# Turning attention probabilities and queries with VectorE and DRAM scratches, in a hybrid SSD and attention trunk

## The chip, the cores and the metric

The kernel runs on one core of one Trainium2 chip. The core has five engines, each with its own instruction queue that is worked off in order: TensorE (PE; its weight loads have a row of their own, PEld), VectorE (DVE), ScalarE (ACT), GpSimd (POOL) and SyncE (SP). DMA transfers are issued from SP, ACT or POOL and run on 16 shared DMA engines. The metric is device time in microseconds; lower is better. The time before is 1022.89 us, the median of three runs (1022.04 to 1023.73).

## The reference

Batch 1, 256 tokens, width 2048, two layers, all in float32. Layer A is a Mamba-2 SSD mixer, layer B a sliding-window attention with grouped queries and a sink for each head. The change is in layer B alone:

```python
proj = x @ w_in                                   # 2048 -> [2048 q | 2048 gate]
q = rope(proj[..., :2048] + q_bias)               # 32 heads of 64; 4 K/V heads, 8 query heads each
k, v = rope(x @ kv_w + kv_b)                      # K and V shared, 4 heads of 64 (rope on k only)
s = einsum("qd,kd->qk", q, [k_prev | k_own]) / 8  # blocks of 128 queries, 256 keys
valid = (diff >= 0) & (diff < 128) & (kpos >= 0)  # diff = query position - key position
m = maximum(max(where(valid, s, -inf)), sink)
p = exp(s - m) / (sum(exp(s - m)) + exp(sink - m))
o = (p @ [v_prev | v_own]) * silu(gate)
x = layernorm(alpha * x + o @ w_out)
```

With 128 queries in a block and a window of 128, query t of a block sees keys 0 to t of its own block and keys t+1 to 127 of the block before: 128 keys in all. The first block has no block before it.

## The kernel before

Products with weights are done in split precision: each float32 weight and activation is split into a high part (float32r) and the rest, and three matmuls (high by high, high by rest, rest by high) are added in PSUM. Weights come in units of 128 partitions by 2048 elements (1 MB), as two DMAs from SP into five raw buffers. `load_unit` (L120) has ScalarE write the high part (L133) and VectorE the rest (L134). `next_unit` (L179) keeps two units ahead of TensorE.

Layer B (from L717) first makes keys and values (`kT`, `vt`), then works through `B_ORDER` (L39), a list of twelve blocks of four units each: "q" (`q_block`, L750: queries of K/V group j, tokens stationary, L712 to L714), "g" (`gate_block`, L778: L195 to L197) and "o" (output projection, `out_unit`, L255 to L257, added to the residual on VectorE at L260 and L264). The last "o" block is run by `out_last`, with the layer norm behind it.

Attention of group j is put between those units by a list of delayed calls: `later(n, fn)` (L201) runs fn at the n-th `tick` (L204) from then, and there is one tick after each unit. Program order sets the order of each engine's queue, except that the Tile scheduler may move an instruction that isn't ready behind others of its engine. The steps for group j and half h (the 128 query tokens of half 0 or 1) are:

- `qtr` (L764), one tick after the q block: four 128 x 128 TensorE transposes (L767) into a PSUM tile `ax`, and a scaled copy to `qT` on ScalarE (L771).
- `attend(j, 0)` (L792), two ticks after the q block, and `attend(j, 1)` three ticks later (one for the last group): scores (L804) of eight heads over nk = 128 (h = 0) or 256 (h = 1) keys; the mask added on VectorE while PSUM is emptied (L809); maximum (L817); eight exponentials with row sums on ScalarE (L823); normalisation (L828).
- `turn_p` (L832), three ticks after `attend`: eight TensorE transposes for h = 0, sixteen for h = 1 (L837), emptied by VectorE (L844) and ScalarE (L842) into tiles `pt`.
- `pv` (L847), one to three ticks later: the product with values (L851), two matmuls of 512 columns for each block of 128 keys, then gate and split (L857, L866, L867) into `oH`, `oL`, which the "o" block of the group uses as stationary operand.

PSUM tiles `ax` have four buffers of one bank. Bias rows are the only DMAs of POOL in these blocks (L690).

Of the kernel before, what the change touches and what calls it, by code (L numbers as in the profile page):

```python
# [38 lines left out]
B_ORDER = [("q", 0), ("g", 0), ("q", 1), ("g", 1), ("o", 0), ("q", 2), ("g", 2), ("o", 1),  # L39
           ("q", 3), ("g", 3), ("o", 2), ("o", 3)]  # L40
# [17 lines left out]
def trunk(ctx: ExitStack, tc: tile.TileContext, A: dict, out: bass.AP, dbg=None):  # L58
# [31 lines left out]
    mask_a1 = cc[:, 640:896]  # L90
# [630 lines left out]
    for h in range(2):  # L721
# [22 lines left out]
        later(2, ktr)  # L744

# [4 lines left out]
    def q_block(j):  # L750
        pss = [mm_tile(), mm_tile()]
        qb = bias_row(A["qb"][j * 512 : (j + 1) * 512])
        for ui in range(4):
            u = next_unit()
            for h in range(2):
                x_stat(pss[h], h, u, ui)
            tick()
        for h in range(2):
            qt = bp.tile([P, 8, 64], F32, tag="qt", name=nm("qt"), bufs=2)
            qf = qt[:].rearrange("p a d -> p (a d)")  # L760
            nc.vector.tensor_tensor(qf, pss[h][:], qb[:], ALU.add)
            rope(qt[:], h, 8)

            def qtr(h=h, qf=qf):  # L764
                pt = ax_tile()
                for p_ in range(4):
                    nc.tensor.transpose(  # L767
                        pt[:, p_ * P : (p_ + 1) * P], qf[:, p_ * P : (p_ + 1) * P], ident
                    )
# [21 lines left out]

    def attend(j, h):  # L792

        nk = P * (h + 1)
        q2 = qT[j, h]
        p = bp.tile([P, 8, nk], F32, tag=f"p{h}", name=nm("p"), bufs=1)
        mask = mask_a1 if h else mask_a0
        per = 512 // nk
        for b in range(0, 4, per):
# [8 lines left out]
            for par in range(2):  # L808
                nc.vector.tensor_tensor(  # L809
                    p[:, par * 4 + b : par * 4 + b + per, :],  # L810
                    pss[par][:].rearrange("p (a k) -> p a k", a=per),
                    mask.unsqueeze(1).to_broadcast([P, per, nk]), ALU.add,
                )
# [14 lines left out]
        nc.vector.tensor_tensor(p[:], p[:], ri.unsqueeze(2).to_broadcast([P, 8, nk]), ALU.mult)  # L828

        pts = {}  # L830

        def turn_p():  # L832
            for kc in range(h + 1):
                for par in range(2):
                    pt = ax_tile()
                    for a in range(4):
                        nc.tensor.transpose(  # L837
                            pt[:, a * P : (a + 1) * P], p[:, par * 4 + a, kc * P : (kc + 1) * P], ident
                        )
                    t = bp.tile([P, 512], F32, tag="pt", name=nm("pt"), bufs=4)  # L840
                    if par:
                        nc.scalar.copy(t[:], pt[:])  # L842
                    else:
                        nc.vector.tensor_copy(t[:], pt[:])  # L844
                    pts[kc, par] = t

        def pv():  # L847
            ov = ax_tile()
            for kc in range(h + 1):
                for par in range(2):  # L850
                    nc.tensor.matmul(  # L851
                        ov[64 * par : 64 * par + 64, :], vt[:, kc, j * 64 : j * 64 + 64], pts[kc, par][:],
# [17 lines left out]
        later(3, turn_p)  # L870
        later(4 if last or h else 6, pv)
# [25 lines left out]
    def done2(h):  # L897
        mv, rs = norm_scale(bp, st2, h)
        if h:
# [7 lines left out]
            for c in range(4):  # L907
# [3 lines left out]
                t = bp.tile([P, 512], F32, tag="pt", name=nm("t"), bufs=4)  # L911
# [11 lines left out]
        for c in range(4):  # L923
            sl = slice(c * 512, (c + 1) * 512)
            v = xr[:, h, sl]
            t = bp.tile([P, 512], F32, tag="pt", name=nm("t"), bufs=4)
# [100 lines left out]
```

## Time and profile before

| what | value |
|---|---|
| time, median of three runs | 1022.89 us |
| span of the profiled execution, first to last instruction | 1022.1 us |
| TensorE matmul / weight load, busy | 1001.7 us (98%) / 905.5 us (89%) |
| VectorE / ScalarE / POOL, busy | 774.2 (76%) / 562.8 (55%) / 89.8 us (9%) |
| mean granted TensorE clock | 0.999 |
| DMA | 199.31 MB, mean 195 GB/s |

The profiled execution's own time is its span of 1022.1 us; the median of the runs is 0.8 us above it. A profile row names line, engine and operation, output tile and input tiles, shape, and count; behind the bar stand busy time and mean duration (ns), and behind the second bar the idle time of the engine just before these instructions and what ended it. In the order of time a row begins with start and duration in us, and "[0.42 <-ACT pt L842]" says that the engine stood idle for 0.42 us until that ScalarE instruction had ended. Matmul durations overlap: a matmul's row lasts from its start to its modelled end, while the next has begun.

### The profile page before, as it was taken

How to read it: one execution, taken by the hardware profiler on the slowest of the kernel's cores; microseconds unless marked ns; L12 is line 12 of the kernel's file. 1: busy time of each engine (PE TensorE's matmuls, PEld its weight loads, DVE VectorE, ACT ScalarE, POOL GpSimd, SP SyncE). 2: the span in 40 equal slices, each digit the busy share in tenths (PEclk: the TensorE clock that was granted, in tenths of full speed). 3: DMA queues.
4: the chain of work that ended last, by engine and by line, in shares of the span. 5: the costliest groups of instructions: out<-in, count | busy, mean ns of one | idle time of the engine just before them, and what ended most of it. 6: DMA issues, size and time to landing. Idle time of an engine off the chain costs nothing. (4 is left out here: it accounts for less than half of the span.)

```text
span 1022.1 us, 17627 instructions
## 1 busy us (share of the span) xinstructions
PE 1001.7 (98%) x7028; PEld 905.5 (89%) x7028; DVE 774.2 (76%) x1106; ACT 562.8 (55%) x924; POOL 89.8 (9%) x112
## 2 busy tenths in 40 slices
PE   7999999999999999999999999999999999999997
PEld 7999899999998998999999999868988879879975
DVE  6868887876886787696786787798577785785776
ACT  6585857637655655664663763535545453453642
POOL 0000303004003002100300300301000000000002
PEclk9999999999999999999999999999999999999999
DMA  8786676575666666656656556647655445545522
GB/s 308 249 299 246 204 245 195 171 233 169 211 218 191 218 195 204 205 188 202 208 179 218 156 190 210 227 146 232 197 167 169 156 140 183 173 140 183 194 96 82
DMA packets 57794, 199.31 MB, mean 195 GB/s; under 512 B 6304, under 2 KB 10672, under 8 KB 56944
## 3 DMA queue, kind: packets, MB, share of 16 engines
q1 hardware_dynamic: 56352, 192.14, 57.3%
q0 software_dynamic: 1072, 5.53, 1.5%
q8 instruction: 55, 0.90, 0.4%
q10 hardware_dynamic: 288, 0.52, 0.1%
q14 instruction: 27, 0.22, 0.1%
HBM read 195.93 MB, written 2.23 MB: 194 GB/s over the span
## 5 line engine op out<-in xcount | busy, mean ns | idle before, releaser
L134 DVE TENSOR_TENSOR wl<-wr,wh 128x1024 fp32r<-128x1024 f32 (+2 forms) x342 | 398.3, 1181 | 135.4 <-ACT wh L133 134.0
L133 ACT ACTIVATE wh<-wr 128x1024 fp32r<-128x1024 f32 (+2 forms) x342 | 337.4, 1011 | 238.9 <-PE mm L196 77.1
L195 PE MATMUL mm<-xH,wh 128*128 128x256 f32 x1296 | 361.2, 279 | 8.0 <-ACT wh L153 6.0
L197 PE MATMUL mm<-xH,wl 128*128 128x256 f32 x1296 | 359.8, 278 | 2.1 <-DVE wl L134 2.1
L196 PE MATMUL mm<-xL,wh 128*128 128x256 f32 x1296 | 360.1, 278 | 0.0
L195 PEld LDWEIGHTS mm<-xH,wh 128*128 128x128 f32 x1296 | 244.6, 189 | 10.2 <-ACT wh L153 6.3
L197 PEld LDWEIGHTS mm<-xH,wl 128*128 128x128 f32 x1296 | 244.5, 189 | 2.7 <-DVE wl L134 2.7
L196 PEld LDWEIGHTS mm<-xL,wh 128*128 128x128 f32 x1296 | 244.7, 189 | 1.1
L255 PE MATMUL mm<-wh,yH 128*128 128x512 f32 x256 | 101.4, 396 | 0.0
L256 PE MATMUL mm<-wh,yL 128*128 128x512 f32 x256 | 99.9, 390 | 0.0
L257 PE MATMUL mm<-wl,yH 128*128 128x512 f32 x256 | 99.7, 390 | 0.0
L492 POOL TENSOR_TENSOR yz<-yz,z 128x256 f32<-128x256 f32 x32 | 32.9, 1036 | 532.0 <-DVE yz L487 532.0
L195 PE MATMUL mm<-x1H,wh 128*128 128x256 f32 x256 | 71.9, 281 | 0.0
L197 PE MATMUL mm<-x1H,wl 128*128 128x256 f32 x256 | 71.0, 277 | 0.0
L196 PE MATMUL mm<-x1L,wh 128*128 128x256 f32 x256 | 71.0, 277 | 0.0
L359 DVE SCALAR_TENSOR_TENSOR cv<-mm,pc,cv 128x255 f32<-128x255 f32 x144 | 68.6, 476 | 1.4
L712 PE MATMUL mm<-wh,x1H 128*128 128x512 f32 x160 | 63.3, 396 | 0.0
L714 PE MATMUL mm<-wl,x1H 128*128 128x512 f32 x160 | 62.6, 392 | 0.3 <-DVE wl L134 0.2
L713 PE MATMUL mm<-wh,x1L 128*128 128x512 f32 x160 | 62.6, 391 | 0.2 <-DVE x1L L676 0.2
L255 PEld LDWEIGHTS mm<-wh,yH 128*128 128x128 f32 x256 | 48.1, 188 | 10.3 <-DVE z L429 1.0
L257 PEld LDWEIGHTS mm<-wl,yH 128*128 128x128 f32 x256 | 48.1, 188 | 10.2
L256 PEld LDWEIGHTS mm<-wh,yL 128*128 128x128 f32 x256 | 48.1, 188 | 9.0
(180 smaller groups left out, 1306.2 us busy)
## 6 DMA issues: line engine op xcount, KB each, us to landing
wr<-in_wa SPq DMA_DIRECT2D x158, 512.0 KB, 5.0
wr<-in_wo SPq DMA_DIRECT2D x64, 512.0 KB, 4.8
wr<-in_wq SPq DMA_DIRECT2D x32, 512.0 KB, 4.5
wr<-in_wg SPq DMA_DIRECT2D x32, 512.0 KB, 5.2
wr<-in_wb SPq DMA_DIRECT2D x32, 512.0 KB, 4.6
rb<-rscr SPq DMA_DIRECT2D x16, 512.0 KB, 5.4
el<-rscr SPq DMA_DIRECT2D x16, 256.0 KB, 4.8
wr<-in_wkv SPq DMA_DIRECT2D x8, 512.0 KB, 4.3
```

Source lines behind the costliest of these rows:

```text
L133: nc.scalar.activation(h[:, sl], raw, AF.Copy)
L134: nc.vector.tensor_tensor(l[:, sl], raw, h[:, sl].bitcast(F32), ALU.subtract)
L195: nc.tensor.matmul(ps, ah, bh, start=first, stop=False)
L196: nc.tensor.matmul(ps, ah, bl, start=False, stop=False)
L197: nc.tensor.matmul(ps, al, bh, start=False, stop=last)
L255: nc.tensor.matmul(ps[:], aH[:, k, hs], u.h[:, ks], start=k == 0, stop=False)
L256: nc.tensor.matmul(ps[:], aL[:, k, hs], u.h[:, ks], start=False, stop=False)
L257: nc.tensor.matmul(ps[:], aH[:, k, hs], u.l[:, ks], start=False, stop=k == 3)
L359: nc.vector.scalar_tensor_tensor(a[:, sft:], ps[:, : S - sft], w(3 - sft), a[:, sft:], ALU.mult, ALU.add)
L712: nc.tensor.matmul(ps[:], x1H[:, kk, hs], u.h[:, ks], start=kk == 0, stop=False)
L713: nc.tensor.matmul(ps[:], x1L[:, kk, hs], u.h[:, ks], start=False, stop=False)
L714: nc.tensor.matmul(ps[:], x1H[:, kk, hs], u.l[:, ks], start=False, stop=kk == KT - 1)
```

## The change

Three things change in layer B.

- *Turning.* Queries and probabilities are no longer transposed by TensorE. VectorE transposes them in blocks of 32 x 32 (`nc.vector.transpose`) into an SBUF tile; four DMAs from POOL, one for each group of 32 partitions, write that to a DRAM scratch (`to_dram`) in an order in which one more DMA from POOL reads it back with keys (or head dimensions) on partitions. The queries' scaled copy on ScalarE then reads the loaded tile instead of PSUM. A call to the loads (`load_q`, `load_p`) comes two ticks behind the stores.
- *128 scores a row in both halves.* For half 1 the scores over 256 keys are still made, but one row of 128 is kept: ScalarE copies the scores of the own block (128 columns), and VectorE overwrites those with key index above the query's by the scores of the block before (`copy_predicated`). Maximum, exponentials and normalisation then run over 128. The value product uses `vt[:, 1] - vt[:, 0]`, formed once: all probabilities by the values of the block before, plus the probabilities masked with `tri` (one multiplication on VectorE) by the difference. The number and the size of its matmuls stay; their moving operand is read in runs of 32 elements.
- *Order and delays.* `B_ORDER` puts q2 ahead of o0 and q3 ahead of o1. `attend(j, 0)` comes four ticks after the q block, `turn_p` two ticks after `attend`, `load_p` four, `pv` six (seven for the last group).

The tiles `p0`, `p1` and `pt` (20 KB a partition together) give way to five buffers of 4 KB under one tag `pb`; temporaries of the last layer norm move from `pt` to the tags `qt` and `qT`.

```diff
-B_ORDER = [("q", 0), ("g", 0), ("q", 1), ("g", 1), ("o", 0), ("q", 2), ("g", 2), ("o", 1),
-           ("q", 3), ("g", 3), ("o", 2), ("o", 3)]
+B_ORDER = [("q", 0), ("g", 0), ("q", 1), ("g", 1), ("q", 2), ("o", 0), ("g", 2), ("q", 3),
+           ("o", 1), ("g", 3), ("o", 2), ("o", 3)]
...
-    mask_a1 = cc[:, 640:896]
+    tri = cc[:, 256:384]
...
+    nc.vector.tensor_tensor(vt[:, 1, :], vt[:, 1, :], vt[:, 0, :], ALU.subtract)
...
-            def qtr(h=h, qf=qf):
-                pt = ax_tile()
-                for p_ in range(4):
-                    nc.tensor.transpose(
-                        pt[:, p_ * P : (p_ + 1) * P], qf[:, p_ * P : (p_ + 1) * P], ident
-                    )
-                q2 = bp.tile([P, 4, P], F32, tag="qT", name=nm("qT"), bufs=2)
-                nc.scalar.activation(
-                    q2[:], pt[:].rearrange("p (a t) -> p a t", a=4), AF.Copy, scale=0.125
-                )
-                qT[j, h] = q2
-
-            later(1, qtr)
+            def turn_q(h=h, qf=qf):
+                z = bp.tile([P, 1024], F32, tag="pb", name=nm("zq"), bufs=5)[:, :512]
+                nc.vector.transpose(
+                    z.rearrange("p (c a t) -> p a c t", c=4, a=4), qf.rearrange("p (a c d) -> p a c d", a=4, c=4)
+                )
+                d = to_dram(z, 128, "qd")
+
+                def load_q():
+                    t = bp.tile([P, 8, 4, 32], F32, tag="pb", name=nm("qr"), bufs=5)[:, :4]
+                    nc.gpsimd.dma_start(t.rearrange("p b a t -> p b (a t)"), d[:].rearrange("b p f -> p b f"))
+                    q2 = bp.tile([P, 4, P], F32, tag="qT", name=nm("qT"), bufs=2)
+                    nc.scalar.activation(
+                        q2[:].rearrange("p a (b t) -> p a b t", b=4), t.rearrange("p b a t -> p a b t"),
+                        AF.Copy, scale=0.125,
+                    )
+                    qT[j, h] = q2
+
+                later(2, load_q)
+
+            later(1, turn_q)
...
+    def to_dram(z, n, name):
+
+        t = dram.tile([4, P, n], F32, tag=name, name=nm(name), bufs=2)
+        for a in range(4):
+            nc.gpsimd.dma_start(
+                t[a, :, :].rearrange("(b t) f -> t b f", b=4),
+                z[32 * a : 32 * a + 32, :].rearrange("p (b f) -> p b f", b=4),
+            )
+        return t
+
     def attend(j, h):
 
+        q2 = qT[j, h]
+        p = bp.tile([P, 8, P], F32, tag="pb", name=nm("p"), bufs=5)
         nk = P * (h + 1)
...
-                nc.vector.tensor_tensor(
-                    p[:, par * 4 + b : par * 4 + b + per, :],
-                    pss[par][:].rearrange("p (a k) -> p a k", a=per),
-                    mask.unsqueeze(1).to_broadcast([P, per, nk]), ALU.add,
-                )
+                v = p[:, par * 4 + b : par * 4 + b + per, :]
+                sv = pss[par][:].rearrange("p (a k) -> p a k", a=per)
+                if h:
+                    nc.scalar.copy(v, sv[:, :, P:])
+                    nc.vector.copy_predicated(
+                        v, mask_a0.bitcast(I32).unsqueeze(1).to_broadcast([P, per, P]), sv[:, :, :P]
+                    )
+                else:
+                    nc.vector.tensor_tensor(v, sv, mask_a0.unsqueeze(1).to_broadcast([P, per, P]), ALU.add)
...
         def turn_p():
-            for kc in range(h + 1):
-                for par in range(2):
-                    pt = ax_tile()
-                    for a in range(4):
-                        nc.tensor.transpose(
-                            pt[:, a * P : (a + 1) * P], p[:, par * 4 + a, kc * P : (kc + 1) * P], ident
-                        )
-                    t = bp.tile([P, 512], F32, tag="pt", name=nm("pt"), bufs=4)
-                    if par:
-                        nc.scalar.copy(t[:], pt[:])
-                    else:
-                        nc.vector.tensor_copy(t[:], pt[:])
-                    pts[kc, par] = t
+            z = bp.tile([P, 1024], F32, tag="pb", name=nm("z"), bufs=5)
+            nc.vector.transpose(
+                z[:].rearrange("p (b h q) -> p h b q", b=4, h=8), p[:].rearrange("p h (b k) -> p h b k", b=4)
+            )
+            held["d"] = to_dram(z, 256, "pd")
+
+        def load_p():
+            t = bp.tile([P, 4, 8, 32], F32, tag="pb", name=nm("pT"), bufs=5)
+            nc.gpsimd.dma_start(t[:].rearrange("p a h q -> p a (h q)"), held["d"][:].rearrange("a p f -> p a f"))
+            held["p"] = [t]
+            if h:
+                m = bp.tile([P, 4, 8, 32], F32, tag="pb", name=nm("pm"), bufs=5)
+                nc.vector.tensor_tensor(
+                    m[:], t[:],
+                    tri.rearrange("p (a q) -> p a q", a=4).unsqueeze(2).to_broadcast([P, 4, 8, 32]), ALU.mult,
+                )
+                held["p"].append(m)
...
-                        ov[64 * par : 64 * par + 64, :], vt[:, kc, j * 64 : j * 64 + 64], pts[kc, par][:],
+                        ov[64 * par : 64 * par + 64, :], vt[:, kc, j * 64 : j * 64 + 64],
+                        held["p"][kc][:, :, 4 * par : 4 * par + 4, :].rearrange("p a h q -> p h a q"),
...
-        later(3, turn_p)
-        later(4 if last or h else 6, pv)
+        later(2, turn_p)
+        later(4, load_p)
+        later(7 if last else 6, pv)
...
-            later(2, lambda j=j: attend(j, 0))
+            later(4, lambda j=j: attend(j, 0))
```

More of the change, by code (lines that the diff above doesn't have):

```diff
@@ L925, in done2 @@
             v = xr[:, h, sl]
-            t = bp.tile([P, 512], F32, tag="pt", name=nm("t"), bufs=4)
+            t = bp.tile([P, 512], F32, tag=("qt", "qT")[c % 2], name=nm("t"), bufs=2)
             nc.vector.scalar_tensor_tensor(
```

9 lines of the change are left out of this document (3 added, 6 removed).

## The prediction

> **What bounds the kernel now.** I read the page first, then the busy times of the stretch from the first gate block of layer B to its last output block, then groups by line, and last the order of time around each interruption of TensorE.
>
> ```profile
> span 1022.1 us, 17627 instructions
> PE 1001.7 (98%) x7028; PEld 905.5 (89%) x7028; DVE 774.2 (76%) x1106; ACT 562.8 (55%) x924; POOL 89.8 (9%) x112
> ...
> 715.80:1011.60 295.80, 294.69 (x1796) 249.83 (x1794) 211.64 (x323) 141.41 (x290) 6.79 (x8) 1.00 0.47 157
> ```
>
> The last row's columns are TensorE, weight loads, VectorE, ScalarE, POOL, granted clock, DMA share, GB/s. In the 295.8 us that the change touches, TensorE lacks 1.1 us of being busy throughout at a granted clock of 1.00; VectorE has 72%, the DMA engines 47%, POOL 2%. So time in layer B is TensorE's issue time, and what leaves TensorE's queue shortens the span unless something becomes late. Layer A keeps its code.
>
> Busy TensorE isn't its price, though: matmuls overlap. The price of a group is the step from its first start to the next group's first start.
>
> ```profile
> 805.55 0.40 PE L255 MATMUL mm<-wh,oH 128*128 128x512 f32 x1
> 811.02 1.03 PE L837 MATMUL ax<-cc,p 128*128 128x128 f32 x8
> 811.99 2.71 PE L804 MATMUL ax<-kT,qT 64*128 64x256 f32 x16
> 813.56 0.73 PEld L804 LDWEIGHTS ax<-kT,qT 64*128 64x128 f32 x6 [0.42 <-ACT pt L842]
> 814.62 0.50 PE L255 MATMUL mm<-wh,oH 128*128 128x512 f32 x1
> ...
> 777.69 1.97 PE L837 MATMUL ax<-cc,p 128*128 128x128 f32 x16
> 779.41 0.37 PE L195 MATMUL mm<-x1H,wh 128*128 128x256 f32 x1
> ...
> 732.26 1.04 PE L767 MATMUL ax<-cc,qt 128*128 128x128 f32 x8
> 733.05 0.36 PE L195 MATMUL mm<-x1H,wh 128*128 128x256 f32 x1
> 738.88 1.16 PE L804 MATMUL ax<-kT,qT 64*128 64x128 f32 x16
> ...
> 953.33 2.00 PE L804 MATMUL ax<-kT,qT 64*128 64x256 f32 x16
> 955.25 0.39 PE L195 MATMUL mm<-x1H,wh 128*128 128x256 f32 x1
> ...
> 973.72 1.53 PE L837 MATMUL ax<-cc,p 128*128 128x128 f32 x12
> 976.22 0.66 PE L837 MATMUL ax<-cc,p 128*128 128x128 f32 x4 [0.96 <-DVE o L857]
> 976.63 0.48 PE L255 MATMUL mm<-wh,oH 128*128 128x512 f32 x1
> ```
>
> A weight unit is 811.02 - 805.55 = 5.47 us of TensorE; one tick of the delay list is one unit.
>
> **What leaves TensorE.**
>
> ```profile
> L837 PE MATMUL ax<-cc,p 128*128 128x128 f32 x96 | 12.2, 275 | 1.0 <-DVE o L857 1.0
> L767 PE MATMUL ax<-cc,qt 128*128 128x128 f32 x32 | 4.2, 274 | 0.0
> L851 PE MATMUL ax<-pt,vt 128*64 128x512 f32 x48 | 12.1, 609 | 0.0
> ```
>
> - The 96 transposes of probabilities (L837). First half, 8 of them: 811.99 - 811.02 = 0.97 us. Second half, 16: 779.41 - 777.69 = 1.72. In the last block the second half takes 976.63 - 973.72 = 2.91, its last four waiting 0.96 for VectorE. With the last block's first half near 0.8 (like the eight at 732.26): 3 x 0.97 + 0.8 + 3 x 1.72 + 2.91 = 11.8 us.
> - The 32 transposes of queries (L767): 733.05 - 732.26 = 0.79 a group, four groups: 3.2 us. The two group rows bear both out: 12.2 + 4.2 busy plus 1.0 idle, less some 0.2 us by which each of twelve groups' last matmul overlaps what follows, is 15.0.
> - Scores of the second half. Directly behind transposes they take 814.62 - 811.99 = 2.63 us, with a wait for the ScalarE copy that frees a PSUM buffer; in the last block, with buffers free, 955.25 - 953.33 = 1.92. The change puts no transposes ahead of them and still does 16 matmuls of 256 columns: 3 x 0.71 = 2.1 us.
> - An interruption less. The unit between queries' transposes and scores takes 738.88 - 733.05 = 5.83 instead of 5.47. About half of the 0.36 I give to the transposes ahead of it (bounds 0 and 0.36): 4 x 0.2 = 0.8 us.
>
> Sum: 11.8 + 3.2 + 2.1 + 0.8 = 17.9 us off TensorE's queue.
>
> By the Trainium skill ("TensorE: Matmul & The Clock Gate", Part 4: PE-mode transpose) a transpose takes about 275 ns in a kernel's context. The mean column here reads 275 and 274 too; by that, 128 of them would be an estimated 35 us and the time near 988. The starts, 0.10 to 0.12 us apart (0.97/8, 1.72/16), decide against it.
>
> **What VectorE and ScalarE get.**
>
> ```profile
> L809 DVE TENSOR_TENSOR p<-ax,cc 128x512 f32<-128x512 f32 x24 | 15.3, 679 | 1.3 <-PE ax L804 1.3
> L817 DVE TENSOR_REDUCE sm<-p 128x8 f32<-128x2048 f32 x4 | 9.1, 2284 | 0.1
> L828 DVE TENSOR_TENSOR p<-p,sm 128x2048 f32<-128x2048 f32 x4 | 9.2, 2290 | 0.1
> L828 DVE TENSOR_TENSOR p<-p,sm 128x1024 f32<-128x1024 f32 x4 | 4.9, 1216 | 0.0
> L844 DVE COPY pt<-ax 128x512 f32<-128x512 f32 x12 | 8.1, 680 | 0.0
> L788 DVE SCALAR_TENSOR_TENSOR sg<-sg,mm 128x256 f32<-128x256 f32 x16 | 6.5, 405 | 1.6 <-ACT sg L787 1.4
> L842 ACT COPY pt<-ax 128x512 f32<-128x512 f32 x12 | 6.5, 574 | 0.0
> L787 ACT ACTIVATE sg<-mm 128x256 f32<-128x256 f32 x16 | 5.9, 367 | 0.0
> L823 ACT ACTIVATE p<-p,sm 128x256 f32<-128x256 f32 x32 | 15.8, 496 | 21.8 <-DVE sm L819 21.8
> L823 ACT ACTIVATE p<-p,sm 128x128 f32<-128x128 f32 x32 | 12.4, 388 | 16.6 <-DVE sm L819 16.6
> ```
>
> VectorE loses L844 (8.1), 16 of the 24 mask additions (16 x 0.679 = 10.9) and half of the 2048-wide reduce and normalisation (9.1/2 + 9.2/2 = 9.2): 28.2 us. No row shows a block transpose or a predicated copy. Nearest by size and type: 1.216 for 1024 elements, 0.680 for 512, 0.405 for 256 out of PSUM. Eight transposes of probabilities, eight of queries, four extra multiplications and 16 predicated copies: 9.7 + 5.4 + 4.9 + 6.5 = 26.5 us; the one subtraction on the values is another 0.4. So VectorE stays near 211 us. At the low end a transpose costs half its row, at the high end four times it (+45 us: 256 of some 279 us, still under TensorE). I take the rows, as size and type agree. ScalarE: minus 6.5 and 32 x 0.108 = 3.5, plus 16 x 0.367 = 5.9. All of this lies beside TensorE.
>
> **What the round trip through DRAM costs.** Each turn issues four stores and one load on POOL: 16 turns, 80 issues, 12.6 MB both ways; with the 46.4 MB of the stretch (157 GB/s x 295.8 us) that is 59 MB in 279 us, 211 GB/s, and layer A ran with TensorE full at such rates.
>
> ```profile
> L690 POOL DMA_DIRECT2D bias<-in_qb x4 | 2.1, 537 | 69.6 <-DVE qt L761 68.9 <-DVE vt L732 0.7
> out<-xr SPq DMA_DIRECT2D x6, 256.0 KB, 2.3
> bias<-in_qb POOLq DMA_DIRECT2D x4, 256.0 KB, 4.6
> wr<-in_wg SPq DMA_DIRECT2D x32, 512.0 KB, 5.2
> ...
> 757.44 1.16 PEld L804 LDWEIGHTS ax<-kT,qT 64*128 64x128 f32 x10 [0.17 <-PE ax L837]
> 769.79 2.28 DVE L828 TENSOR_TENSOR p<-p,sm 128x2048 f32<-128x2048 f32 x1
> ...
> 982.26 1.94 PE L851 MATMUL ax<-pt,vt 128*64 128x512 f32 x8
> 986.11 0.68 DVE L867 TENSOR_TENSOR oL<-o,oH 128x512 fp32r<-128x512 f32 x1
> ```
>
> An issue took 0.54 us on POOL, a store of 256 KB landed after 2.3, loads of 256 and 512 KB after 4.6 and 5.2. The store and load shapes are new; bounds are 0.54 for an issue with as many pieces as the bias row and 2.1 for a load with four times the pieces, landing of a store 2.3 to 4.6. I take 0.54 and the longer landing.
>
> - Probabilities, turn to use: transpose 1.2, four issues 2.2, landing 4.6, issue 0.5, landing 5.2, multiplication 1.2: 14.9 us against four ticks, 21.9. Hidden.
> - Queries of blocks 0 and 3, turn to first score: transpose 0.7, eight issues 4.3 (both halves' stores stand ahead of the load), rest of the landing 2.4, issue 0.5, landing 4.6, ScalarE 0.6 (L787's and L842's rows): 13.1 against three ticks, 16.4. Hidden.
> - Queries of blocks 1 and 2 queue on POOL behind the previous block's second half, turned at the same tick. Its probabilities were ready 769.79 + 2.28 - 757.44 = 14.6 us after the scores' start, now 3.0 earlier (1.1 each for reduce and normalisation, as L828's two rows differ, and 8 x 0.108): 11.6, or 6.1 after the query block's end. Transpose to 7.3, twelve issues to 13.8, two load issues to 14.9, landing 4.6 to 7.2 (half a 512 KB load beside it), ScalarE 0.6: 20.1 to 22.7 against four ticks plus the values' matmuls between (4 x 12.1 / 48 = 1.0), 22.9. That just fits; with long load issues (2.1) it is 3 us late. I take 0.5 each, 1.0 us in all (bounds 0 and 6).
> - The last block's second half now reaches its values' matmuls one unit later, directly ahead of the last output block. Before, L867 ended at 986.79, 2.6 us after those matmuls (982.26 + 1.94); the output block has 2.7 us of first-half matmuls to do meanwhile. I take 0.3 (bounds 0 and 1.5, one weight split in front).
>
> What waits behind a late load: on ScalarE the queries' copy, on VectorE the multiplication, each with weight splits behind it that TensorE reads two units (10.9 us) later; a wait of a few microseconds stays inside that.
>
> Sum: 17.9 - 1.0 - 0.3 = 16.6 us. Profiled span 1022.1 - 16.6 = 1005.5; the median of the runs shown, 1022.89, lies 0.8 above that span, so **1006.3 us**.
>
> **Rivals.**
> - *Part of the gain is eaten* by queries that come late for blocks 1 and 2 and a stall at the last output block: the upper bounds above, 6 + 1.5 instead of 1.3, make 1012.5. For it: new shapes of DMA, the thin margin. Against it: VectorE runs ahead of the ticks where nothing holds it. It takes 2.4 times that lateness (17.9 / 7.5) to reach no change.
> - *POOL's queue becomes the bound: slower than before.* If each issue waits out the VectorE instruction under way (1.22 us, the L828 row), it costs 1.76: twelve stores and two loads for blocks 1 and 2 take 14 x 1.22 = 17.1 us more, less at most 2.8 of margin, so 14 us or more late twice; blocks 0 and 3 take ten issues, 12.2 more less 3.3, 8.9 late twice. That is +46 on -17: 1051. It turns into a loss at some 0.55 us more an issue (2 x (14 x 0.55 - 2) + 2 x (10 x 0.55 - 3.3) = 16). Against it: all bias rows were issued in 0.54 beside a VectorE at 72%. The Trainium skill ("SBUF — State Buffer", Who interferes with whom) says that VectorE in a two-port mode shuts POOL out of SBUF while it writes descriptors, and gives 3.1 us instead of 0.62 for such a DMA; no row here shows a large instruction of that kind beside a POOL issue, so whether the block transpose is one stays open.
> - *The values' matmuls read slower*, as they now take runs of 32 elements with gaps in place of 512 in a row. At twice the 12.1 us of L851 the time is 1018.4; the loss begins at 2.4 times. No row speaks for it.
> - *Nothing moves*: the transposes' slots turn into waits of the same length for data that comes through DRAM, 1022.9. Against it stand the margins above.
>
> **How the numbers follow.** No change means within 0.2%, 1020.8 to 1024.9, about what a measurement of this kernel can tell. The forecast (1003 to 1009) has 0.62, the eaten gain 0.17, the slower reads 0.03, nothing moved 0.05, POOL's queue 0.13. Faster is 0.62 + 0.17 + 0.03 = 0.82, same 0.05, slower 0.13. The lower end of the range, 1003, is the whole 17.9 with up to 2 us more from interruptions that go; the upper end, 1018, takes in the eaten gain and slower reads.
>
> **What would show it.** L837 and L767 gone, 6900 matmuls; scores of the second half near 1.9 us each; TensorE still above 99% busy in layer B, with waits before L804 of blocks 1 and 2 under 1 us; POOL issues of 0.5 us, VectorE's transposes near 1.2 and 0.7. Wrong if TensorE waits for the ScalarE copy of the queries or for the loaded probabilities by more than 5 us together, or if POOL's issues take over 1 us.

## The result and the profile after

The changed kernel takes **1010.73 us** (median of four runs, 1009.90 to 1011.93) against 1022.75 (1022.04 to 1023.73, four runs beside it). The ratio is 0.9885 with a 95% interval of 0.9871 to 0.9899: 12.0 us faster. The forecast was 1006.3, its range 1003 to 1018. Line numbers below are those of the changed kernel: scores L821, value products L876, queries' copy L776, the multiply `pm` L866, gate and rounding of the result L883, L892, L893, stores L804, loads L862 (probabilities) and L774 (queries), block transposes L855 and L767.

From the page of the changed kernel:

```profile
span 1010.1 us, 17539 instructions
...
PE 989.0 (98%) x6900; PEld 891.8 (88%) x6900; DVE 772.3 (76%) x1115; ACT 558.9 (55%) x928; POOL 138.1 (14%) x192
```

The 128 transposes are gone (7028 matmuls before). The profiled execution took 1011.93 us, the slowest of the four; its span is 12.0 us below that of the kernel before, as the medians are. Where the time went is read from three stretches of layer B, cut at starts on TensorE: the first transpose of the keys, the start of the unit behind the last gate matmul, the first matmul of the tail. Columns as in the prediction's first windows row; the third number is the length. The kernel before:

```profile
715.02:960.82 245.80, 245.66 (x1574) 211.70 (x1572) 171.59 (x272) 120.63 (x251) 1.07 (x2) 1.00 0.50 164
960.82:1011.59 50.77, 49.81 (x230) 38.90 (x228) 40.33 (x53) 21.56 (x40) 5.71 (x6) 1.00 0.35 124
1011.59:1022.12 10.53, 3.97 (x9) 1.34 (x8) 5.82 (x10) 2.07 (x5) 1.10 (x1) 0.90 0.43 156
```

The changed kernel:

```profile
713.98:947.22 233.24, 232.03 (x1470) 199.04 (x1468) 169.74 (x283) 119.15 (x272) 44.41 (x76) 1.00 0.65 213
947.22:998.81 51.59, 48.18 (x206) 36.23 (x205) 39.91 (x50) 19.12 (x24) 9.42 (x12) 1.00 0.48 180
998.81:1010.12 11.31, 5.46 (x9) 1.62 (x8) 5.81 (x10) 2.07 (x5) 1.11 (x1) 0.79 0.38 145
```

The long stretch became 12.6 us shorter. The next one, the last **output stretch**, holds 24 transposes fewer (x230 to x206) and still grew by 0.8 us: TensorE now lacks 3.4 us of being busy in it, before 1.0. The tail took 0.8 us more, at a granted clock of 0.79 instead of 0.90; over the fourteen kernels of this study it takes 10.3 to 10.6 us where its clock is 0.89 or more, and 10.6 to 11.3 where it is 0.60 to 0.81. Layer A ended 1.0 us earlier; over the same fourteen, whose layer A is the same, layer B began between 711.7 and 715.4, so that one is chance. Of the forecast 16.6 us, 4.6 are missing, and the output stretch, which was to become some 3 us shorter and didn't, is where most of them went. The order of time on TensorE there:

```profile
968.17 0.50 PE L255 MATMUL mm<-wh,oH 128*128 128x512 f32 x1 [0.48 <-DVE xr L264]
...
971.12 1.08 PE L876 MATMUL ax<-pT,vt 128*64 128x512 f32 x4
972.03 1.03 PE L876 MATMUL ax<-pm,vt 128*64 128x512 f32 x4
974.03 0.49 PE L255 MATMUL mm<-wh,oH 128*128 128x512 f32 x1 [0.97 <-ACT oH L892]
975.10 0.50 PE L256 MATMUL mm<-wh,oL 128*128 128x512 f32 x1 [0.58 <-DVE oL L893]
...
978.69 0.49 PE L255 MATMUL mm<-wh,oH 128*128 128x512 f32 x1 [0.81 <-ACT oH L892]
979.77 0.50 PE L256 MATMUL mm<-wh,oL 128*128 128x512 f32 x1 [0.58 <-DVE oL L893]
```

The last value products end, and the last output block, which reads their gated and rounded result, waits four times: first for the first half's `oH` and `oL`, then for the second half's (2.9 us in all). The other 0.5 us came a unit earlier, in a wait for a sum on VectorE that frees TensorE's PSUM. VectorE in the same time:

```profile
963.68 0.68 DVE L264 TENSOR_TENSOR xr<-xr,mm 128x512 f32<-128x512 f32 x1
966.29 1.22 DVE L866 TENSOR_TENSOR pm<-pT,cc 128x1024 f32<-128x1024 f32 x1 [1.93 <-DMA pT<-pd]
967.43 0.68 DVE L264 TENSOR_TENSOR xr<-xr,mm 128x512 f32<-128x512 f32 x1
968.03 2.35 DVE L134 TENSOR_TENSOR wl<-wr,wh 128x1024 fp32r<-128x1024 f32 x2
970.30 1.27 DVE L264 TENSOR_TENSOR xr<-xr,mm 128x512 f32<-128x512 f32 x2
971.50 1.21 DVE L134 TENSOR_TENSOR wl<-wr,wh 128x1024 fp32r<-128x1024 f32 x1
972.63 0.68 DVE L883 SCALAR_TENSOR_TENSOR o<-ax,sg 128x512 f32<-128x512 f32 x1
```

VectorE stood still 1.93 us at the multiply `pm` of the second half, which waits for the load of the turned probabilities, and had 6.3 us of work (972.63 - 966.29) from there to the gate of the first half, whose matmuls had ended by 964.7. And POOL, which issues that trip through DRAM:

```profile
950.14 2.19 POOL L804 DMA_DIRECT2D pd<-z  x4 [0.26 <-DVE z L855]
952.32 0.56 POOL L920 DMA_DIRECT2D gb<-in_lng  x1
958.71 0.76 POOL L862 DMA_DIRECT2D pT<-pd  x1 [5.83 <-DMA pd<-z]
```

The stores' last issue ended at 952.3, their landing let the load go at 958.7, and it landed at 966.3 (VectorE's row above). Between the two POOL issued a 1 MB row of the last layer norm, and the second such row behind the load. (The kernel before issues these two rows from POOL as well, at 961.2 and 961.7 us, so the bias rows are not POOL's only DMAs there; its DMA share from 955 to 970 was 0.59.) From 955 to 970 us the DMA engines are full:

```profile
935.00:945.00 10.00, 10.00 (x91) 10.00 (x90) 7.87 (x15) 6.47 (x25) 2.19 (x4) 1.00 0.21 49
945.00:955.00 10.00, 10.00 (x57) 8.65 (x56) 9.24 (x13) 7.30 (x13) 3.50 (x6) 1.00 0.82 256
955.00:965.00 10.00, 10.00 (x44) 7.40 (x43) 5.39 (x7) 3.18 (x3) 1.30 (x2) 1.00 1.01 407
965.00:970.00 5.00, 4.52 (x20) 3.41 (x19) 3.71 (x4) 2.10 (x2) 0.00 (x0) 1.00 1.02 422
```

The column before the last is the DMA share: 0.21, 0.82, 1.01, 1.02. So four things meet there: late probabilities, VectorE's queue behind them, full DMA engines, and value products directly ahead of the block that reads their result. The experiments take them apart as far as they could.

### The profile page after: what moved, and what is told of

Same layout as the page of the kernel before. It is cut to its first block, busy times and chain, and to the rows that moved or that the text cites. A ratio compares the mean times of both kernels' runs of the same rounds, so it can differ in the third digit from the quotient of the medians.

```text
span 1010.1 us, 17539 instructions
## 1 busy us (share of the span) xinstructions
PE 989.0 (98%) x6900; PEld 891.8 (88%) x6900; DVE 772.3 (76%) x1115; ACT 558.9 (55%) x928; POOL 138.1 (14%) x192
## 4 chain that ended last, share of the span: by engine, by line
PE 73%; DVE 11%; DMA 6%; ACT 5%; issue 3%; POOL 2%; SPq 0%; DVEq 0%; POOLq 0%; ACTq 0%
PE mm L195 13%; PE mm L196 13%; PE mm L197 13%; PE mm L255 6%; PE mm L256 6%; PE mm L257 6%; DVE wl L134 4%; PE mm L712 3%; PE mm L713 3%; PE mm L714 3%; ACT wh L133 2%; PE ax L476 2%; DMA wr<-in_wa 2%; DVE cv L359 1%; PE ax L821 1%
## 5 line engine op out<-in xcount | busy, mean ns | idle before, releaser
L255 PE MATMUL mm<-wh,yH 128*128 128x512 f32 x256 | 101.4, 396 | 0.0
L255 PEld LDWEIGHTS mm<-wh,yH 128*128 128x128 f32 x256 | 48.1, 188 | 10.3 <-DVE z L429 1.0
```

The source lines that it names most:

```text
L255: nc.tensor.matmul(ps[:], aH[:, k, hs], u.h[:, ks], start=k == 0, stop=False)
```

## The experiments

All twelve, with the three stretches of their profiled execution. "Ratio" is to the kernel before, in runs on the same chip.

| kernel | time us | ratio, 95% interval | long | output | tail |
|---|---|---|---|---|---|
| before | 1022.75 | | 245.8 | 50.8 | 10.5 |
| changed | 1010.73 | 0.9885 [0.9871, 0.9899] | 233.2 | 51.6 | 11.3 |
| norm rows late | 1011.07 | 0.9886 [0.9867, 0.9905] | 232.7 | 50.6 | 10.8 |
| values early | 1010.01 | 0.9872 [0.9854, 0.9891] | 233.5 | 49.9 | 11.0 |
| both | **1006.65** | 0.9841 [0.9823, 0.9860] | 232.6 | 47.7 | 10.6 |
| queries' load a tick earlier | 1015.43 | 0.9926 [0.9908, 0.9945] | 238.8 | 50.7 | 11.3 |
| queries on TensorE | 1010.19 | 0.9880 [0.9855, 0.9904] | 235.5 | 47.1 | 11.3 |
| both, queries on TensorE | 1008.99 | 0.9868 [0.9846, 0.9890] | 235.5 | 47.0 | 10.3 |
| dead transposes | 1024.32 | 1.0016 [1.0005, 1.0026] | 248.1 | 50.1 | 10.5 |
| both, dead transposes | 1022.89 | 0.9997 [0.9984, 1.0011] | 246.0 | 47.0 | 10.3 |
| splits first | 1011.24 | 0.9886 [0.9868, 0.9904] | 232.0 | 52.3 | 11.3 |
| `pm` on GpSimd | 1010.95 | 0.9886 [0.9867, 0.9904] | 233.1 | 50.4 | 10.6 |
| before, 128 scores alone | 1016.80 | 0.9943 [0.9925, 0.9961] | 243.2 | 48.8 | 11.0 |
| before, values late | 1021.16 | 0.9985 [0.9975, 0.9994] | 245.8 | 49.7 | 11.3 |

### Norm rows late

```diff
-    nc.gpsimd.dma_start(gb2[0][:], A["lng"][1].partition_broadcast(P))
-    nc.gpsimd.dma_start(gb2[1][:], A["lnb"][1].partition_broadcast(P))
...
+    def stats2(h, nb):
+        norm_stats(st2, h, nb)
+        if (h, nb) == (0, 1):
+            for i, name in enumerate(("lng", "lnb")):
+                tc.keep_in_program_order(nc.sync.dma_start(gb2[i][:], A[name][1].partition_broadcast(P)))
+
-    out_last(*os_[3], None, lambda h, nb: norm_stats(st2, h, nb), done2)
+    out_last(*os_[3], None, stats2, done2)
```

> The changed kernel, with the two loads of the last layer norm's rows (2 MB, issued from POOL behind the probabilities' DMAs, on the wire from about 952 us) issued from SP behind the last weight unit. In the changed kernel TensorE stands idle for some 4.4 us between 967 and 980 us. Theory A (these 2 MB fill the DMA engines just when the last weights and the last probabilities have to land, so VectorE runs late and the output block waits for it): the DMA share in 955 to 970 us falls from 1.00 to about 0.7, ScalarE's waits for the last weight units go, TensorE's idle time there falls from 4.4 to under 1 us, time 1006 to 1007.5. Theory B (the last value products stand one unit later and the order of VectorE's queue makes them late whatever the DMAs do): idle time stays 3 us or more, time 1009.5 to 1011.

The probabilities landed at 964.1, 2.2 us earlier, but the time did not move (1011.07). The four waits for `oH` and `oL` went; another came in their place, one unit ahead. Its row on TensorE:

```profile
966.04 0.52 PE L255 MATMUL mm<-wh,oH 128*128 128x512 f32 x1 [1.86 <-DVE xr L264]
966.35 0.63 PE L256 MATMUL mm<-wh,oL 128*128 128x512 f32 x1
```

TensorE waits for a PSUM buffer that VectorE has yet to empty, since VectorE stands at `pm` (idle for 2.89 us until its load had landed at 964.07), and the sum comes right behind. The matmuls behind it then came 0.43 apart instead of 0.23, at a granted clock of 0.57 from 966 to 970. The DMA share from 955 to 970 fell from 1.01 to 0.79, near the 0.7 that the first theory expected, but up to 963 the engines stay full (1.02 and 1.03): these rows were only a part of that load.

### Values early

```diff
-        later(7 if last else 6, pv)
+        later(6, pv)
```

> The changed kernel, with the last group's value products one unit earlier (delay six instead of seven). Theory A (crowded DMA engines): the loaded probabilities of the second half land only at about 966 us, so TensorE now waits for them instead, 3 to 4 us before the value products; time 1009.5 to 1012. Theory B (only the place in the order): the output block finds its operands ready, time 1006 to 1007.5.

1010.01, as the theory of crowded DMA engines expected. Here the wait is for the load itself, and only 0.26 us is left behind it:

```profile
967.42 1.08 PE L876 MATMUL ax<-pT,vt 128*64 128x512 f32 x4 [2.37 <-DMA pT<-pd]
968.76 1.08 PE L876 MATMUL ax<-pm,vt 128*64 128x512 f32 x4 [0.26 <-DVE pm L866]
```

Either edit alone moves the wait to the next link: the sums, or the load.

### Both

The two edits together.

> The changed kernel, with the layer-norm rows loaded behind the last weight unit AND the value products of the last block one place earlier, each of which alone left about 2 us of wait at another place. Theory A (VectorE's late splits and the bunched weights remain): a wait of 1 to 2.5 us moves to the splits of the last output weights or to the sums of the output block, stretch 49 to 50 us, time 1008 to 1010. Rival D (the two late transfers are all of it): no wait over 0.3 us left in the last output block, stretch 47 to 47.5 us, time about 1006.

**1006.65 us** (1005.26 to 1008.00), the fastest kernel of this study; the interval of its ratio doesn't touch that of the changed kernel. The output stretch fell from 51.6 to 47.65 us; what the first theory expected (a wait that moves on, 1008 to 1010) did not come. TensorE:

```profile
963.11 1.08 PE L876 MATMUL ax<-pT,vt 128*64 128x512 f32 x4 [0.19 <-DMA pT<-pd]
964.33 1.08 PE L876 MATMUL ax<-pm,vt 128*64 128x512 f32 x4
965.34 0.50 PE L255 MATMUL mm<-wh,oH 128*128 128x512 f32 x1
```

VectorE:

```profile
963.05 1.23 DVE L866 TENSOR_TENSOR pm<-pT,cc 128x1024 f32<-128x1024 f32 x1 [3.69 <-DMA pT<-pd]
964.20 1.28 DVE L264 TENSOR_TENSOR xr<-xr,mm 128x512 f32<-128x512 f32 x2
965.39 1.22 DVE L134 TENSOR_TENSOR wl<-wr,wh 128x1024 fp32r<-128x1024 f32 x1
966.52 0.69 DVE L883 SCALAR_TENSOR_TENSOR o<-ax,sg 128x512 f32<-128x512 f32 x1
```

VectorE waits longer at `pm` than in the changed kernel (3.69 us), and it costs nothing: the gate comes 3.5 us behind the landing, and an output unit (965.34 to 970.94) now lies between the value products and the first reader of `oH`.

### Before, values late

Is the place alone the price? The same place in the kernel before, where nothing goes through DRAM:

```diff
-        later(4 if last or h else 6, pv)
+        later(5 if last else 4 if h else 6, pv)
```

> The kernel before, with one edit: the value products of the last block one place later, so that those of its second half stand directly ahead of the last output block, as in the changed kernel (in the kernel before one output unit of 5.45 us lay between). Nothing of that block goes through DRAM here. Theory F (the place costs little while VectorE's queue is not held up): no wait for oH or oL over 0.5 us, time 1022.3 to 1023.5. Rival G (the place alone costs about 3 us): the stretch from the last gate matmul to the tail grows from 50.8 to 53 to 54 us, time 1025 to 1026.

No wait, and 1021.16 us: a little faster than before, since the value products of the last first half no longer stand between the transposes of the second half (their PSUM wait of 0.96 us is gone). TensorE goes straight on:

```profile
984.14 1.94 PE L851 MATMUL ax<-pt,vt 128*64 128x512 f32 x8
986.00 0.50 PE L255 MATMUL mm<-wh,oH 128*128 128x512 f32 x1
```

In the kernel before, where VectorE reaches the gate in time, the place costs nothing. The rival with the place alone falls there.

### Splits first

```diff
+            if len(units) >= len(srcs) - 12:
+                with tc.high_priority(300):
+                    units.append(load_unit(srcs[len(units)], places))
```

> The changed kernel, with one edit: the loads and splits of the last 12 weight units get a higher priority with the planner, so that VectorE's queue has two weight splits ahead of each reciprocal of the last group's two halves (where it idled 3.2 and 2.2 us waiting for ScalarE's exponentials). No work is added or removed. Theory A (VectorE's order in the last group holds the raw weight buffers, the transfers bunch up at 955 to 970 us, and TensorE waits for them): the stretch from the last gate matmul to the tail shrinks from 51.6 to 47 to 48 us, the time falls to about 1006.5. Rival B (the DMA engines are full at 955 to 970 whatever the order, with layer-norm rows, probabilities and weights together): the stretch stays above 50.5 us and the time within 1.5 us of 1010.7. Rival C (the later normalisation and transpose of the probabilities make the last value products late): a wait of TensorE for pT or oH/oL of over 2 us, time 1010 to 1014.

1011.24. VectorE's queue did change as meant (two weight splits ahead of each reciprocal of the last group), and the waits for sums went, but the first half's gate was late all the same (the added lines shift the numbers here: L260 is L255, L897 is L892):

```profile
972.69 0.79 PE L260 MATMUL mm<-wh,oH 128*128 128x512 f32 x1 [2.36 <-ACT oH L897]
```

VectorE waited 5.76 us at `pm`, whose load landed at 966.7, again with sums and splits queued between it and the gate (971.3). So the theory that late splits were the cause falls. Both rivals fit by their figures: the wait for `oH` is over 2 us, and the DMA engines were as full as before from 955 to 965 (1.03 and 1.02), with the stretch at 52.3 us. This run doesn't tell them apart.

### `pm` on GpSimd

```diff
-                nc.vector.tensor_tensor(
+                (nc.gpsimd if last else nc.vector).tensor_tensor(
                     m[:], t[:],
```

> The changed kernel, with one edit: in the last block the multiply of the turned probabilities by the triangle (pm) runs on GpSimd instead of VectorE, everything at its old place. In the changed kernel VectorE waited 1.93 us at this multiply for the load of p and took 1.14 us for it, with weight splits, sums and the first half's gate queued behind it; the gate came 6.3 us after the load landed. Theory F (VectorE's queue, held up at pm, makes the gated values late): the first half's gate comes about 3 us earlier, at 969 to 970 us, the waits for oH and oL shrink to under 1 us together, the last stretch falls from 51.6 to 48 to 49 us, time 1007 to 1008.5. Rival G (the place alone: the last value products stand directly ahead of the output block that reads them, and the gate, its rounding and its rest cost TensorE 3 us there whatever VectorE did before): stretch 50.5 us or more, time 1010 to 1011.

1010.95, and **inconclusive**: VectorE was not set free. GpSimd:

```profile
964.93 2.39 POOL L867 TENSOR_TENSOR pm<-pT,cc 128x1024 f32<-128x1024 f32 x1 [6.38 <-DMA pT<-pd]
```

VectorE beside it:

```profile
963.71 4.70 DVE L134 TENSOR_TENSOR wl<-wr,wh 128x1024 fp32r<-128x1024 f32 x2
968.33 1.27 DVE L264 TENSOR_TENSOR xr<-xr,mm 128x512 f32<-128x512 f32 x2
```

Two splits take 2.35 us in the changed kernel; here they took 4.70, the second alone 3.3, with the multiply on GpSimd over it. The gate came at 970.7, 5.7 us behind the landing where it had been 6.3, and the waits for `oH` and `oL` stayed (2.5 us in all). That VectorE's stand at `pm` is the link that matters is therefore argued from the order of time, not shown by an edit of its own.

### Queries on TensorE

In the changed kernel, and then in the version with both edits; the queries are transposed and copied as in the kernel before, probabilities go through DRAM.

```diff
-            def turn_q(h=h, qf=qf):
...
-            later(1, turn_q)
+            def qtr(h=h, qf=qf):
+                pt = ax_tile()
+                for p_ in range(4):
+                    nc.tensor.transpose(pt[:, p_ * P : (p_ + 1) * P], qf[:, p_ * P : (p_ + 1) * P], ident)
...
+            later(1, qtr)
```

> The changed kernel, with the queries turned by TensorE again (32 transposes, as before the change), probabilities still through DRAM. By the prediction's terms TensorE gets 3.2 us of transposes and 0.8 of interruptions back and loses the 1.3 us of waits for late queries: time 1010.7 + 2.7 = 1013.4. The rival, that the scratch path's waits eat what turning queries gains: no change or faster, 1010 to 1011.

> The version with late norm rows and early value products (1006.65), with the queries turned by TensorE again as in the kernel before (32 transposes, no DRAM trip for them). In the changed kernel the same step left the time where it was (1010.19 against 1010.73). Theory A (there the 3.4 us that TensorE lost were given back by the wait at the end, and now there is no wait to give anything back): the stretch from layer B's start to the last gate matmul grows by 2.5 to 3.5 us, the last one stays at 47 to 48 us, time 1009 to 1010. Rival E (turning the queries through DRAM gains nothing anywhere, its waits at the scores take it back): time within 1 us of 1006.65.

In the changed kernel it made no difference to the time (1010.19), as the rival expected: the long stretch grew by 2.3 us, the output stretch fell by 4.5. So the two became 2.2 us shorter together; layer A, which ended 1.4 us later in that execution, hides most of it. The stretches of the first:

```profile
715.38:950.87 235.49, 235.49 (x1501) 202.51 (x1500) 168.55 (x280) 121.21 (x275) 22.89 (x40) 1.00 0.60 197
950.87:997.99 47.12, 47.12 (x207) 36.32 (x205) 36.09 (x46) 16.57 (x20) 7.57 (x9) 1.00 0.46 180
```

TensorE is without a gap in both, although the value products keep their late place and the norm rows their early one. The last scores began 3.7 us later (932.5 against 928.8), the probabilities landed 0.8 us earlier (965.5 against 966.3): VectorE and the DMA engines were no later, and TensorE came late enough not to wait. With both edits the same step cost 2.9 us in the long stretch, 0.6 came back in the output stretch, and the time was 1008.99 against 1006.65, close to what the first theory expected. The intervals of those two ratios overlap, so the traces carry this, more than the times.

### Dead transposes

128 TensorE transposes of a constant put back where the stores to DRAM are called, in the changed kernel and in the version with both edits.

```diff
+    def dead_turns(n):
+        for _ in range(n):
+            pt = ax_tile()
+            for a in range(4):
+                nc.tensor.transpose(pt[:, a * P : (a + 1) * P], ident, ident)
```

> The changed kernel, with 128 TensorE transposes of a constant added where probabilities and queries are stored to DRAM (4 per half of a query block, 8 and 16 per first and second half of scores): TensorE's queue gets back what the change took from it, nothing reads the results. If TensorE sets the pace everywhere: 128 x 0.1225 us = 15.7 us more, about 1026. Theory A (at the end TensorE waits some 4.4 us for a chain that it does not set, and is given that back when it comes later): 11 to 12 us more, 1022, with the stretch from the last gate matmul to the tail not longer than 52 us though 1.5 to 3 us of dead transposes lie in it.

> The version with late norm rows and early value products (1006.65), with the 128 dead TensorE transposes added that made the changed kernel 13.6 us slower (14.9 us in the stretch up to the last gate matmul, 1.5 us back behind it). Theory A (nothing to give back): 14.5 to 15.5 us more, 1021 to 1022, the last stretch stays at 47 to 48 us. Rival (VectorE or the DMA still set part of the pace in this version): 13 us more or less, below 1020.

13.6 us more in the changed kernel (1024.32), between the two expectations; 16.2 in the other (1022.89), by the profiled executions 14.0 (1019.27 against 1005.26), by the long and the output stretch together 12.8. The median lies above both expectations for that version, the stretches fit the rival's figure, so it decides nothing between them. All 128 stand in the long stretch (1597 matmuls against 1469). The version with both edits gives the better price, as TensorE has no gap left with them in it:

```profile
713.84:959.87 246.03, 246.03 (x1597) 212.87 (x1596) 173.97 (x288) 121.54 (x275) 46.92 (x81) 1.00 0.64 206
959.87:1006.88 47.01, 47.01 (x206) 36.38 (x204) 35.09 (x45) 16.22 (x20) 5.75 (x6) 1.00 0.48 178
```

246.03 - 232.59 = 13.4 us for 128 transposes, 0.105 us each; without them TensorE lacked 0.6 us there (231.99 busy), so its busy time grew by 14.0, 0.11 us each. In the changed kernel the long stretch took 14.9 us more, two waits on VectorE among them (0.78 and 0.81 us), and the output stretch gave only 1.5 back. So it isn't simply that TensorE runs ahead of a chain that it doesn't set: there the chain moved with TensorE (last scores 8.7 us later, landing 9.3 later).

### Queries' load a tick earlier

```diff
-                later(2, load_q)
+                later(1, load_q)
```

> The changed kernel, with the queries' load one tick behind their stores instead of two: POOL issues it ahead of the previous block's load of probabilities. The prediction's step said that queries of blocks 1 and 2 come 0.5 us late each; the trace shows 0.9 us before the scores of block 1, none at block 2 and 0.4 inside those of block 3. If POOL's order makes that wait, it goes at block 1 (time 0.5 to 1.2 us less: 1009.5 to 1010.2). If the wait is for landing under crowded DMA engines, it stays: 1010.7. ScalarE may in return stand in front of its weight splits waiting for the load; if that reaches TensorE the time rises by 1 us or more.

The wait of 0.82 us for block 1's queries went, and the kernel lost 4.7 us (1015.43): in the last group TensorE waited 4.66 us for a sum on VectorE, which stood behind a weight split that waited for ScalarE:

```profile
924.74 0.63 ACT L776 ACTIVATE qT<-qr 128x512 f32<-128x512 f32 x1 [2.50 <-DMA qr<-qd]
...
926.35 1.23 DVE L134 TENSOR_TENSOR wl<-wr,wh 128x1024 fp32r<-128x1024 f32 x1 [2.99 <-ACT wh L133]
927.49 1.28 DVE L264 TENSOR_TENSOR xr<-xr,mm 128x512 f32<-128x512 f32 x2
...
928.23 0.58 PE L195 MATMUL mm<-x1H,wh 128*128 128x256 f32 x1 [4.66 <-DVE xr L264]
```

ScalarE stood at the copy of the last group's queries until their load had landed, and wrote the weights' high parts only then. This is the risk that the expectation named. The same chain stands in the changed kernel some 5 us earlier (the split at 921.28, behind it a wait of TensorE of 0.30 us). The delay is first seen on VectorE at `pm` of the group before: it began at 900.91 instead of 896.05, VectorE having stood idle for 8.7 us instead of 5.8. The load of those probabilities was issued at 894.8 instead of 890.6; why POOL came to it later stays open. So it is the same kind of link at other places: an instruction on VectorE or ScalarE that waits for DRAM, and behind it a sum that frees TensorE's PSUM.

### Before, 128 scores alone

The second part of the change put into the kernel before by itself, with TensorE's transposes and the old order.

> The kernel before, with only the 128-score part: the second half keeps 128 probabilities a row (own block of keys, or the earlier block by predicated copy), they are turned by TensorE as before (8 transposes fewer in each second half), masked products multiply values that have the first half subtracted. If the terms of the prediction hold alone (32 transposes x 0.1225 = 3.9, scores of the second halves 2.1): 6 us less, about 1016.9. Rival (the copy on ScalarE, the predicated copy and the second product take back on VectorE and ScalarE what TensorE saves, since TensorE then waits for them): 2 us or less, 1021 or more.

6.4 us faster by the medians (1016.80 against 1023.20 beside it), about what was worked out from the prediction's terms; the long and the output stretch became 4.6 us shorter. So 4.6 to 6.4 of the changed kernel's 12.0 us need no DRAM.

Not tried, and so open: what the new order of blocks is worth by itself.

## Why the prediction was nearly right, and where it failed

**What leaves TensorE: right.** The transposes' steps summed to 11.77 and 3.24 us in the trace of before and are gone; the scores fell from 14.28 to 12.43 us in all, 1.93 for each second half where 1.92 was forecast. These are 16.9 us of the forecast 17.1; the 0.8 for interruptions wasn't measured by itself. The dead transposes price the same 128 at 13.4 to 14.0 us, some 0.11 us each. The 275 ns of the Trainium skill ("TensorE: Matmul & The Clock Gate", Part 4: PE-mode transpose) are what one lasts, as in the mean column of before, and not what it costs the queue here.

**VectorE and ScalarE: right.** The new operations, from the groups by line and shape of layer B:

```profile
L804 POOL DMA_DIRECT2D pd<-z x32 | 17.5, 554 | 110.7 <-DVE z L855 73.6 <-DVE sm L839 24.3 <-DVE qt L705 12.9
...
L855 DVE STREAM_TRANSPOSE z<-p 128x1024 f32<-128x1024 f32 x8 | 9.9, 1236 | 0.0
...
L862 POOL DMA_DIRECT2D pT<-pd x8 | 6.1, 758 | 36.4 <-DMA pd<-z 30.0 <-ACT sg L795 5.5 <-DMA qd<-zq 0.9
L774 POOL DMA_DIRECT2D qr<-qd x8 | 6.0, 754 | 18.2 <-DMA qd<-zq 11.9 <-issue 6.2
L830 DVE COPY_PREDICATED p<-cc,ax 128x256 f32<-128x256 int32 x16 | 5.9, 438 | 0.2 <-ACT p L829 0.2
...
L767 DVE STREAM_TRANSPOSE zq<-qt 128x512 f32<-128x512 f32 x8 | 5.4, 697 | 0.1
```

1.236 and 0.697 us for the block transposes (1.216 and 0.680 taken), 0.438 for the predicated copy (0.405). VectorE was busy for 169.7 + 39.9 = 209.6 us in the first two stretches, forecast near 211. POOL's issues took 0.55 us for stores and 0.76 for loads: the **rival with POOL's queue** falls. The stores at 778.4 and 830.6 us and the load at 949.1 overlapped with block transposes on VectorE, and took no longer than the others. None came near the 3.1 us that the Trainium skill gives for such a DMA beside a VectorE copy ("SBUF — State Buffer", A bandwidth-pool intuition that's wrong).

**Queries: the mechanism right.** Block 1 waited 0.82 us for the copy of its queries, block 2 not at all, against 0.5 each. The **slower reads** fell too: four value products took 1.01 us and eight 1.87, as before.

**The time lies between the forecast and the rival in which part of the gain is eaten** (1012.5), which had 0.17, and outside the 1003 to 1009 us that had 0.62. Of that rival the stall at the last output block came true, beyond its bound of 1.5 us; the late queries, its larger part, did not, so its time comes this near by luck. TensorE was busy for 98.4% of the first two stretches (280.2 of 284.8 us) where over 99% was to be seen. The waits that the prediction named as its sign of being wrong, for the queries' copy or for the loaded probabilities, came to 0.8 us: the loss lay in waits that it had not listed.

**The failed step** is "I take 0.3 (bounds 0 and 1.5, one weight split in front)" for the last block's second half directly ahead of the last output block. It measured about 4 us: 51.6 against 47.65 us of output stretch with both edits. Two things were wrong in it. It counted the way of the second half's gate alone, with 2.7 us of first-half matmuls as cover; but the first half's gate was late as well, behind 6.3 us of work in VectorE's queue, so that this cover itself stood still. And the sentence that a late load on VectorE delays only weight splits that TensorE reads two units later left out what else stands in that queue: the sums that free PSUM, and the gate. That VectorE's stand at `pm` is what delays the gate is read from the order of time; the run that was to isolate it was inconclusive. "Hidden" for the probabilities was true for TensorE (landed at 966.3, read at 971.1) and not for VectorE. The round trip was longer than taken, too: 17.7 us from the start of the block transpose (948.6) to landing against 13.7 by the prediction's terms (14.9 without the multiplication). From the last store's issue to the load's issue it was 6.4 us instead of 4.6, and the load landed after 6.8 instead of 5.2. For the load that is no more than the median of all eight (6.9), so the full DMA engines at the end don't explain it.

With that step mended the sum holds: from the keys' transposes to the tail the version with both edits takes 232.59 + 47.65 = 280.2 us against 296.6 before, 16.3 less where 16.6 was forecast, and its time is 1006.65 where 1006.3 was. That the two times meet within 0.4 us is in part luck, as the runs of that version spread over 2.7 us.

**What stays open**: which of the causes made the last probabilities land late (VectorE's own place, the full DMA engines, the queries' traffic). With the queries on TensorE they landed 33.0 us after the start of the last scores, in the changed kernel 37.5; the runs don't tell why.

## What to carry to other kernels

When work leaves the engine that bounds the kernel and comes back by DMA, follow the load into the queue of every engine that reads it: an instruction that waits there holds up all that stands behind it, also what the bounding engine needs from something else. Count the distance from a product to its reader from the last thing in that queue, and leave a unit of other work between them. If a removed cost shows up as a wait at one place, move that wait on purpose: here each of two edits alone only passed it to the next link, and both together removed it.

## What the runs showed of the hardware

- A wait of TensorE of 1.86 us was followed by half the clock. Behind it, in the kernel with late norm rows, the granted clock was 0.57 from 966 to 970, which is 3.4 us at half, and matmuls came 0.43 us apart instead of 0.23. Behind 2.36 us in the kernel with splits first it was 0.57 from 972 to 976; behind 2.37 us in the kernel with early values it stayed at 1.00. The Trainium skill ("TensorE: Matmul & The Clock Gate", Part 1) ties the drop to an idle window of about 3.4 us that runs freely. The 3.4 us that the slow clock lasted agree; that 1.86 us can be enough doesn't.
- The 128x1024 multiply with both inputs in SBUF took 2.39 us on GpSimd, and a VectorE split of the same size beside it, 1.22 us elsewhere, took 3.3. In that run, offloading to GpSimd moved the time and didn't save it.
- Stores of 64 and 128 KB from POOL to DRAM landed after a median of 4.1 and 4.8 us, loads of 256 and 512 KB after 6.3 and 6.9, about the longest that had been assumed for the stores (4.6) and 1.7 us more for the loads.
